# Another order of side streams and gates in a one-core layer kernel with attention, S5 and RG-LRU

## The chip, the cores and the metric

The kernel runs on one core of a Trainium2 chip. The metric is the device time of one execution in microseconds. Three runs of the kernel before gave 1795.3, 1797.18 and 1800.35 us; the median is 1797.18. Less time is better.

## The reference

One decoder layer for 2048 prompt tokens and 32 sample tokens (8 sequences of 4), all in float32, with 1024 features. One projection feeds three mixers and their gates:

```
q, k, v, g_a, u_b, g_b, x_c, g_c, g_m = split(x @ w_in)
attn = sliding-window attention(q, k, v)      # window 128, 8 query heads, 2 kv heads, sinks, bias
y_b  = S5(u_b); y_b = y_b * sigmoid(y_b @ w_glu)
y_c  = RG-LRU(causal conv4(x_c))
ya = (attn * silu(g_a)) @ w_br_a              # and yb, yc in the same way
merged = sum of sigmoid(g_m parts) * (ya, yb, yc)
y = LayerNorm(alpha * x + merged @ w_out) * ln_g + ln_b
```

The outputs are y and the new caches and states of the three mixers, for prompt and sample.

## The kernel before

**First phase.** The projection is done in 50 tiles of 128 output features: u (4), x (4), k, v, q (4), m (24, the merge gates), then the branch gates gc, gb and ga (4 each). Each tile has five units over the 2080 tokens: three of 512 columns and two of 272. A unit takes 8 slices of 128 input features, and each slice is three matmuls (mm3, lines 98 to 101), since every factor is split into a high and a low part. The result lies in a PSUM buffer mm, of which there are three. evac (line 192) empties it: for most tiles ScalarE copies it, through tanh for m, into a buffer st of the ring stage (three buffers of 128 x 512), and ScalarE's queue stores it to DRAM. For a gate tile ScalarE takes the tanh into gt, VectorE multiplies by PSUM (the first stt) and then by the mixer's output br, which gate_load (line 1371) has fetched one unit ahead, and the result in st is stored by SP's queue at the start of the next unit. gt (two buffers) and br (three) lie in a pool named gate, which attention's stream opens when it begins.

**Side streams.** The mixers are generators. tick (line 151) adds 3n/2400 to a pace after each slice of n columns; when the pace has reached the price of the last step, the next step of the first stream in the list is emitted, and the pace begins at zero. A step without a price of its own costs STEP = 4.6. All engines work in the order in which the instructions are emitted. S5 comes first; when the x tiles begin, GLU (on S5's output yD, to zD), RG-LRU (from xD, to hD) and attention (from qD, kD and vD, to aD) are appended in this order. Before gc the loop waits until attention's stream has begun, before ga until its prompt part is done, and at unit 3 of the first ga tile until all streams are done.

RG-LRU goes through four groups of 128 channels with nine steps each: five with matmuls, then Exp, Tanh, and a step with Sqrt on ScalarE and, behind it, two long multiplies and the scan on VectorE, after which SP stores hD and two states; one step is empty. GLU has eight pairs of steps, each step with 24 matmuls.

**Second phase.** The three gated branches are multiplied by their matrices (y_unit, line 1446, PSUM buffers py, four), weighted by the merge gates and summed in acc; the output projection and LayerNorm follow. BR gives the order of the branches, "cba". In the last gate branch of the first phase, seam (line 1339) fetches and splits the first branch's values (act_load, act_split) for the second phase: per unit, two raw tiles come from the pool z1 and two from stage.

**Start.** x is loaded in tiles of 128 x 512 into the ring xr (six buffers), split by ScalarE and VectorE, and kept in SBUF.

Of the kernel before, what the change touches and what calls it, by code (L numbers as in the profile page):

```python
# [9 lines left out]
FT = mybir.dt.float32  # L10
# [18 lines left out]
STEP = 4.6  # L29
# [5 lines left out]
TILES = ([("u", i) for i in range(4)] + [("x", i) for i in range(4)] + [("k", 0), ("v", 0)]  # L35
         + [("q", i) for i in range(4)]
         + [("m", i) for i in range(24)]
         + [("gc", i) for i in range(4)] + [("gb", i) for i in range(4)] + [("ga", i) for i in range(4)])
IN_NAMES = ["xT", "xr", "w_in", "w_br", "w_out", "w_glu", "lru_w", "lru_v", "lru0", "conv0",
            "s5p", "s5b", "s5c", "s5cd", "s5h", "s5hx", "s5d", "relT", "sinks", "ckT", "ck", "cv", "lnp"]  # L40
OUT_SPECS = [("y", (T, 1024)), ("kvp", (2, 128, 128)), ("ssm_p", (128, 32)), ("lru_p", (128, 4)),
# [12 lines left out]
def kernel(ctx: ExitStack, tc: tile.TileContext, I, O):  # L54
# [7 lines left out]
    def uid(p):  # L62
        cnt[0] += 1
        return f"{p}{cnt[0]}"
# [23 lines left out]
    def act(out, in_, func, scale=1.0, bias=0.0, **kw):  # L88
        return A.activation(out, in_, func, bias=bias, scale=scale, **kw)  # L89
# [24 lines left out]
    ph1 = ctx.enter_context(ExitStack())  # L114
    xlp = ph1.enter_context(tc.tile_pool(name="xl", bufs=1))
    wpool = ph1.enter_context(tc.tile_pool(name="wp", bufs=2))
    stage = ph1.enter_context(tc.tile_pool(name="stage", bufs=3))
    psum = ph1.enter_context(tc.tile_pool(name="psum", bufs=1, space=PSUM))

    def side_pool(es, name, bufs=1):  # L120
        return es.enter_context(tc.tile_pool(name=name, bufs=bufs, side="right", reuse_waits="tile"))
# [13 lines left out]

    sides, a_done, prompt_done, pace, hold = [], [False], [False], [0.0, STEP], [0]

    def side_step():  # L140
        while sides:
            try:
                r = next(sides[0])
                if r == "a":
                    a_done[0], r = True, None
                return STEP if r is None else r
            except StopIteration:
                sides.pop(0)
        return 1e9
# [42 lines left out]
    def evac(kind, i, u, ps):  # L192
        t0, n = UN[u]
        if kind == "u":
            if u == 0:
                US[i] = early.tile([128, 8, 272], FT, name=uid("us"), tag="us", bufs=2)
                G.memset(US[i][:, :, 256:272], 0.0)
            us = US[i]
            c0, nch = t0 // 8, min(n, TP - t0) // 8
            act(us[:, :, c0:c0 + nch], ps[:, :nch * 8].rearrange("p (c j) -> p j c", j=8), AF.Copy)  # L200
            if u == 4:
                smp = ps[:, 240:272].rearrange("p (b t) -> p t b", t=4)
                act(us[:, 0:4, 256:264], smp, AF.Copy)
                act(us[:, 4:8, 264:272], smp, AF.Copy)
                ST.dma_start(uD[i], us)
        elif kind == "x":
            spill(ps, n, xD[i][:, t0:t0 + n])
        elif kind in "kv":
            st = spill(ps, n, (kD if kind == "k" else vD)[:, t0:t0 + n])
            if u == 4:  # L210
                ST.dma_start(O["kvp"][0 if kind == "k" else 1], st[:, 112:240])
        elif kind == "q":
            spill(ps, n, qD[i][:, t0:t0 + n])
        elif kind == "m":
            spill(ps, n, mD[i][:, t0:t0 + n], AF.Tanh, 0.5)
        else:
            b = kind[1]
            gt = gp[0].tile([128, 512], FT, name=uid("gt"), tag="gt", bufs=2)[:, :n]
            br = gate_br.pop((b, i, u))
            act(gt, ps[:, :n], AF.Tanh, scale=0.5)  # L220
            stt(gt, gt, 1.0, ps[:, :n], OP.add, OP.mult)
            st = stage.tile([128, 512], FT, name=uid("st"), tag="st")[:, :n]
            if b == "b":
                nch = min(n, TP - t0) // 8
                V.tensor_mul(st[:, :nch * 8].rearrange("p (c j) -> p c j", j=8),
                             gt[:, :nch * 8].rearrange("p (c j) -> p c j", j=8),
                             br[:, :, 0:nch].rearrange("p j c -> p c j"))
                if u == 4:
                    V.tensor_mul(st[:, 240:272].rearrange("p (b t) -> p b t", t=4),
                                 gt[:, 240:272].rearrange("p (b t) -> p b t", t=4),  # L230
                                 br[:, 0:4, 30:38].rearrange("p t b -> p b t"))
            else:
                V.tensor_mul(st, gt, br)
            gate_st.append((actD[b][i][:, t0:t0 + n], st))
# [690 lines left out]


    def attn_stream():
        gp.append(side_pool(ges, "gate"))
        es = ExitStack()
        p = side_pool(es, "attn")  # L930
        sk = p.tile([128, 10], FT, name="sk")
# [188 lines left out]
        for n in range(34):  # L1120
            b, kv = divmod(n, 2)
# [23 lines left out]
                        load(b + 2)  # L1145
            yield ATT_SOFTMAX
        es.close()
        prompt_done[0] = True

        es = ExitStack()  # L1150
        p2 = side_pool(es, "attns")
# [74 lines left out]
        for b_ in range(8):  # L1226
            c = slice(b_ * 16, b_ * 16 + 16)
            PE.matmul(pv[:, :, b_], vc[:, b_], PT[:, :, c], start=b_ == 0, stop=False, skip_group_check=True)
        for b_ in range(8):
            c = slice(b_ * 16, b_ * 16 + 16)  # L1230
# [12 lines left out]
    early = side_pool(ees, "early")  # L1243
# [3 lines left out]
    def x_load(u):  # L1247
        t0, n = UN[u]
        for k in range(8):
            if u == 0 and k % 2 == 0:  # L1250
                kk = slice(k, k + 2)
                LD.dma_start(WR[0][:, kk], I["w_in"][0][:, kk])
            xr = early.tile([128, 512], FT, name=uid("xr"), tag="xr", bufs=6)
            LD.dma_start(xr[:, :n], I["xT"][k * 128:k * 128 + 128, t0:t0 + n])
            if u == 0 and k % 2 == 0:
                split(WS[0][0][:, kk], WS[0][1][:, kk], WR[0][:, kk])
            split(X[u][0][:, k], X[u][1][:, k], xr[:, :n])
# [1 line left out]
    x_load(0)  # L1259
    WS[1] = tuple(wpool.tile([128, 8, 128], FR, name=uid("w1"), tag=t) for t in ("wh", "wl"))  # L1260
    for kk in (slice(0, 4), slice(4, 8)):
        r = early.tile([128, 512], FT, name=uid("xr"), tag="xr", bufs=6).rearrange("p (k c) -> p k c", k=4)
        LD.dma_start(r, I["w_in"][1][:, kk])
        split(WS[1][0][:, kk], WS[1][1][:, kk], r)
    w_load(2)
# [13 lines left out]
    gp = []  # L1279
    ges = ExitStack()  # L1280


    BR = "cba"
    SCL = {"a": 0.5, "b": 0.125, "c": 0.5}
    MB = {"a": 0, "b": 8, "c": 16}
    ACT_, WB, WR2, TH, AR = {}, {}, {}, {}, {}
# [12 lines left out]
    def act_load(bi, c, k, st=False):  # L1299
        t0, n = UN[c]  # L1300
        r = raw_tile(bi == 0, st)[:, :n]
        AR[bi, c, k] = r
        LD.dma_start(r, actD[BR[bi]][k][:, t0:t0 + n])

    def act_split(bi, c, k):
# [9 lines left out]
        t = ACT_[bi, c]  # L1315
        split(t[k], t[4 + k], AR.pop((bi, c, k)), SCL[BR[bi]])

    def wb_load(j):
        if j < 24:
            bi, m = divmod(j, 8)  # L1320
            WR2[bi, m] = r = z1[0].tile([128, 4, 128], FT, name=uid("wbr"), tag="wbr", bufs=1)
            LD.dma_start(r, I["w_br"]["abc".index(BR[bi]), m])

# [8 lines left out]
    def th_load(bi, m, c, tag="br"):  # L1332
        t0, n = UN[c]
        TH[bi, m, c] = th = gp[0].tile([128, 512], FT, name=uid(tag), tag=tag, bufs=3 if tag == "br" else 2)[:, :n]
        LD.dma_start(th, mD[MB[BR[bi]] + m][:, t0:t0 + n])

# [31 lines left out]

    gate_br, gate_st = {}, []

    def gate_load(b, i, u):
        t0, n = UN[u]
        br = gp[0].tile([128, 512], FT, name=uid("br"), tag="br", bufs=3)
        if b == "b":
            c0, nch = t0 // 8, 38 if u == 4 else n // 8
            br = br[:, :8 * nch].rearrange("p (j c) -> p j c", j=8)
            LD.dma_start(br, zD[i][:, :, c0:c0 + nch])
        else:
            br = br[:, :n]
            LD.dma_start(br, (hD if b == "c" else aD)[i][:, t0:t0 + n])  # L1380
        gate_br[(b, i, u)] = br

    UORD = [3, 4, 0, 1, 2]
    for i in range(2, len(TILES)):
        kind, ti = TILES[i]
        if kind == "x" and ti == 0:
            while not a_done[0]:
                side_step()
            ees.close()
            hold[0] = 0  # L1390
            sides += [glu_stream(), lru_stream(), attn_stream()]
        if kind == "gc":
            while not gp:
                side_step()
        if kind == "ga":
            while not prompt_done[0]:
                side_step()
        if kind[0] == "g" and ti == 0:
            gate_load(kind[1], ti, 0)
        order = UORD if i == len(TILES) - 1 else list(range(5))  # L1400
        for p, u in enumerate(order):
            while gate_st:
                LD.dma_start(*gate_st.pop(0))
            if (kind, ti, p) == ("ga", 0, 3):
                while sides:
                    side_step()
            if kind[0] == "g" and (p < 4 or ti < 3):
                nxt = order[p + 1] if p < 4 else UORD[0] if i == len(TILES) - 2 else 0
                gate_load(kind[1], ti + (p == 4), nxt)
            ps = gemm(i, u)  # L1410
            if p == 0:
                w_split(i + 1)
            if p == 1:
                w_load(i + 2)
            evac(kind, ti, u, ps)
            if kind == "ga":
                seam(ti, u)
            hold[0] = int(a_done[0] and kind == "u")
            tick(UN[u][1])
# [139 lines left out]
    gb = lnp.tile([128, 2, 1024], FT, name="lngb")  # L1559
# [108 lines left out]
```

## Time and profile before

| | |
|---|---|
| median of three runs | 1797.18 us |
| the profiled execution's own time | 1798.88 us |
| its span, first to last instruction | 1797.1 us |
| mean granted TensorE clock | 0.997 |
| TensorE busy, matmuls | 1775.0 us (99%) |
| TensorE weight loads | 1549.5 us (86%) |
| VectorE busy | 1130.8 us (63%) |
| ScalarE busy | 653.8 us (36%) |
| GpSimd busy | 167.9 us (9%) |
| DMA | 220.36 MB, mean 123 GB/s |

Busy time of TensorE is the union of its matmuls' records, whose ends are modelled and overlap. Time that an engine sat idle is given before an instruction, with what released it. SP's queue issues most loads; ACTq is ScalarE's own queue of DMAs. The granted clock is 1.00 at 2.4 GHz and near 0.5 at 1.2 GHz.

### The profile page before, as it was taken

The numbers are of one execution on the slowest core, as the hardware profiler recorded it, in microseconds if no ns is written. First come the engines' busy times: TensorE is split into PE (matmuls) and PEld (weight loads), VectorE is DVE, ScalarE is ACT, GpSimd is POOL, SyncE is SP. The second block draws the span as 40 slices with busy tenths as digits, with TensorE's granted clock in tenths as the row PEclk, the third lists the DMA queues.
The fourth block names the chain that finished last, engine by engine and source line by source line (L and its number), as shares of the span: only waits on it lengthen the run. The fifth ranks groups of instructions, "written<-read, shape, count | busy, mean of one in ns | idle before, by whom it ended". The sixth has DMA issues, their size and how long they took to land. (4 is left out here: it accounts for less than half of the span.)

```text
span 1797.1 us, 26615 instructions
## 1 busy us (share of the span) xinstructions
PE 1775.0 (99%) x9788; PEld 1549.5 (86%) x9788; DVE 1130.8 (63%) x2450; ACT 653.8 (36%) x1382; POOL 167.9 (9%) x377
## 2 busy tenths in 40 slices
PE   8999999999999999999999999999999999999998
PEld 7888888888899888888988888888888888888886
DVE  5755888886334456653777899654343557666666
ACT  6312443343333287674565655311220202111110
POOL 0000000000000000000355555400000000000000
PEclk9999999999999999999999999999999999999999
DMA  7443333433333334443332334453455646542222
GB/s 235 111 135 100 111 109 112 116 108 92 120 120 114 101 93 123 104 103 95 103 104 85 119 120 134 106 165 101 143 176 155 185 137 189 186 140 94 94 94 77
DMA packets 214038, 220.36 MB, mean 123 GB/s; under 512 B 89125, under 2 KB 156709, under 8 KB 212741
## 3 DMA queue, kind: packets, MB, share of 16 engines
q1 hardware_dynamic: 182532, 169.27, 33.2%
q10 hardware_dynamic: 31376, 49.39, 7.8%
q8 instruction: 77, 1.26, 0.3%
q14 instruction: 53, 0.43, 0.1%
HBM read 136.53 MB, written 83.14 MB: 122 GB/s over the span
## 5 line engine op out<-in xcount | busy, mean ns | idle before, releaser
L99 PE MATMUL mm<-xh,wh 128*128 128x512 f32 (+1 forms) x1920 | 678.9, 354 | 0.0
L101 PE MATMUL mm<-xh,wl 128*128 128x512 f32 (+1 forms) x1920 | 673.5, 351 | 0.0
L100 PE MATMUL mm<-xl,wh 128*128 128x512 f32 (+1 forms) x1920 | 671.4, 350 | 0.0
L101 PEld LDWEIGHTS mm<-xh,wl 128*128 128x128 f32 x1920 | 361.5, 188 | 47.0 <-DVE wl L94 0.3
L99 PEld LDWEIGHTS mm<-xh,wh 128*128 128x128 f32 x1920 | 362.0, 189 | 43.4
L100 PEld LDWEIGHTS mm<-xl,wh 128*128 128x128 f32 x1920 | 362.1, 189 | 42.9
L99 PE MATMUL py<-ah,wbh 128*128 128x512 f32 (+1 forms) x480 | 168.9, 352 | 1.5 <-DVE acc L104 1.5
L101 PE MATMUL py<-ah,wbl 128*128 128x512 f32 (+1 forms) x480 | 168.9, 352 | 0.0
L100 PE MATMUL py<-ah,wbh 128*128 128x512 f32 (+1 forms) x480 | 168.8, 352 | 0.0
L89 ACT ACTIVATE st<-mm 128x512 f32<-128x512 f32 (+1 forms) x170 | 86.9, 511 | 157.2 <-PE mm L101 146.2
L99 PEld LDWEIGHTS py<-ah,wbh 128*128 128x128 f32 x480 | 90.2, 188 | 14.7 <-issue 1.9
L100 PEld LDWEIGHTS py<-ah,wbh 128*128 128x128 f32 x480 | 90.3, 188 | 12.8
L101 PEld LDWEIGHTS py<-ah,wbl 128*128 128x128 f32 x480 | 90.2, 188 | 12.5
L94 DVE TENSOR_TENSOR wl<-wr,wh 128x1024 fp32r<-128x1024 f32 x48 | 58.9, 1226 | 38.1 <-ACT wh L89 38.0
L104 DVE SCALAR_TENSOR_TENSOR gt<-gt,mm 128x512 f32<-128x512 f32 (+1 forms) x60 | 35.0, 584 | 71.1 <-ACT gt L89 70.9
L104 DVE SCALAR_TENSOR_TENSOR br<-br,py 128x512 f32<-128x512 f32 (+1 forms) x80 | 46.9, 586 | 50.9 <-PE py L101 42.5
L89 ACT ACTIVATE gt<-mm 128x512 f32<-128x512 f32 (+1 forms) x60 | 30.9, 515 | 114.4 <-PE mm L101 114.4
L89 ACT ACTIVATE wbh<-wbr 128x512 fp32r<-128x512 f32 x24 | 15.1, 629 | 147.7 <-PE py L100 125.6
L89 ACT ACTIVATE wh<-wr 128x1024 fp32r<-128x1024 f32 x48 | 50.5, 1052 | 23.8 <-DMA wr<-in_w_in_dram 14.5
L104 DVE SCALAR_TENSOR_TENSOR zy<-zs,zy 128x528 f32<-128x528 f32 x16 | 11.3, 709 | 75.4 <-ACT zs L89 75.4
L104 DVE SCALAR_TENSOR_TENSOR acc<-br,py 128x512 f32<-128x512 f32 (+1 forms) x38 | 22.1, 588 | 46.2 <-PE py L101 37.8
L1492 PE MATMUL po<-woh,mg 128*128 128x512 f32 x128 | 49.8, 389 | 0.0
(347 smaller groups left out, 2916.5 us busy)
## 6 DMA issues: line engine op xcount, KB each, us to landing
wr<-in_w_in_dram SPq DMA_DIRECT2D x48, 512.0 KB
mD<-st ACTq DMA_DIRECT2D x72, 256.0 KB
br<-mD SPq DMA_DIRECT2D x71, 256.0 KB
lx<-in_xr_dram SPq DMA_DIRECT2D x16, 512.0 KB
mD<-st ACTq DMA_DIRECT2D x48, 136.0 KB
br<-mD SPq DMA_DIRECT2D x47, 136.0 KB
xr<-in_xT_dram SPq DMA_DIRECT2D x24, 256.0 KB
wbr<-in_w_br_dram SPq DMA_DIRECT2D x24, 256.0 KB
```

What stands on the lines that cost most here:

```text
L89: return A.activation(out, in_, func, bias=bias, scale=scale, **kw)
L94: V.tensor_sub(lo, src, hi)
L99: PE.matmul(ps, wh, xh, start=start, stop=False)
L100: PE.matmul(ps, wh, xl, start=False, stop=False)
L101: PE.matmul(ps, wl, xh, start=False, stop=stop)
L104: return (eng or V).scalar_tensor_tensor(out, a, s, b, op0=op0, op1=op1)
L1492: PE.matmul(ps[c], h[:, k, :rows], wh, start=k == 0, stop=False)
```

## The change

The list of streams is now attention, RG-LRU, GLU (S5 is still ahead of them), and the gate tiles come as ga, gc, gb. BR, the order of branches in the second phase, is "acb", so that the first branch there is again that of the gates done first. Before the first ga tile at most two streams may be left, before gc one, before gb none. gb is now the branch beside which the seam runs.

The pool gate is opened only when gb begins. Until then, gate_tile takes br and gt from the ring stage, and the product is written into gt itself, in place of a tile st. stage has four buffers instead of three, and xr five instead of six.

```diff
-         + [("gc", i) for i in range(4)] + [("gb", i) for i in range(4)] + [("ga", i) for i in range(4)])
+         + [("ga", i) for i in range(4)] + [("gc", i) for i in range(4)] + [("gb", i) for i in range(4)])
...
-    stage = ph1.enter_context(tc.tile_pool(name="stage", bufs=3))
+    stage = ph1.enter_context(tc.tile_pool(name="stage", bufs=4))
...
-            gt = gp[0].tile([128, 512], FT, name=uid("gt"), tag="gt", bufs=2)[:, :n]
+            early_ = not gp
+            gt = gate_tile("gt")[:, :n]
             br = gate_br.pop((b, i, u))
             act(gt, ps[:, :n], AF.Tanh, scale=0.5)
             stt(gt, gt, 1.0, ps[:, :n], OP.add, OP.mult)
-            st = stage.tile([128, 512], FT, name=uid("st"), tag="st")[:, :n]
+            st = gt if early_ else stage.tile([128, 512], FT, name=uid("st"), tag="st")[:, :n]
...
     def attn_stream():
-        gp.append(side_pool(ges, "gate"))
...
-            xr = early.tile([128, 512], FT, name=uid("xr"), tag="xr", bufs=6)
+            xr = early.tile([128, 512], FT, name=uid("xr"), tag="xr", bufs=5)
...
-    BR = "cba"
+    BR = "acb"
...
+    def gate_tile(tag):
+
+        if not gp:
+            return stage.tile([128, 512], FT, name=uid("st"), tag="st")
+        return gp[0].tile([128, 512], FT, name=uid(tag), tag=tag, bufs=3 if tag == "br" else 2)
+
     def gate_load(b, i, u):
         t0, n = UN[u]
-        br = gp[0].tile([128, 512], FT, name=uid("br"), tag="br", bufs=3)
+        br = gate_tile("br")
...
-            sides += [glu_stream(), lru_stream(), attn_stream()]
-        if kind == "gc":
-            while not gp:
+            sides += [attn_stream(), lru_stream(), glu_stream()]
+        if kind[0] == "g" and ti == 0:
+
+            while len(sides) > {"a": 2, "c": 1, "b": 0}[kind[1]]:
                 side_step()
-        if kind == "ga":
-            while not prompt_done[0]:
-                side_step()
+            if kind == "gb":
+                gp.append(side_pool(ges, "gate"))
...
-            if (kind, ti, p) == ("ga", 0, 3):
-                while sides:
-                    side_step()
...
-            if kind == "ga":
+            if kind == "gb":
                 seam(ti, u)
```

## Rows read from the trace of the kernel before

**Rows 1.** Windows: stretch, length, busy us (instructions) per engine, clock, DMA share, GB/s.

```profile
850.00:875.00 25.00, 23.55 (x137) 20.98 (x136) 16.66 (x47) 14.20 (x43) 3.45 (x7) 0.93 0.40 126
875.00:1015.00 140.00, 139.66 (x858) 125.19 (x857) 106.98 (x235) 86.34 (x266) 76.20 (x151) 1.00 0.30 94
1015.00:1175.00 160.00, 154.33 (x906) 135.88 (x905) 133.09 (x271) 78.30 (x239) 78.51 (x154) 0.99 0.43 127
1250.00:1330.00 80.00, 80.00 (x439) 70.38 (x438) 31.20 (x55) 20.18 (x39) 0.00 (x0) 1.00 0.48 153
```

**Rows 2.** TensorE's waits, 1015 to 1175: us in total, times, longest.

```profile
PE sc L1052 <- DVE S L1012: 2.4, 4, 1.1
PE sb L1100 <- POOL ptl L1082: 1.8, 3, 1.2
PE sb L1100 <- POOL pth L1082: 0.7, 1, 0.7
PE sc L1052 <- ACT oo L89: 0.7, 1, 0.7
```

**Rows 3.** Timeline of TensorE: start, duration, instruction, idle before it; GLU and seam.

```profile
511.06 0.29 PE L99 MATMUL sa<-zh,gluh 128*128 128x264 f32 x1
...
1337.00 0.39 PE L101 MATMUL py<-ah,wbl 128*128 128x512 f32 x1
1338.88 0.47 PE L99 MATMUL py<-ah,wbh 128*128 128x512 f32 x1 [1.50 <-DVE acc L104]
```

**Rows 4.** Windows, just after the seam's wait.

```profile
1340.00:1342.00 2.00, 2.00 (x11) 1.59 (x10) 0.44 (x1) 0.00 (x0) 0.00 (x0) 1.00 0.82 208
```

**Rows 5.** Instructions on tile gt: duration ns min/median/max, first and last start, forms.

```profile
L104 DVE SCALAR_TENSOR_TENSOR gt<-gt,mm x60: 416/678/690, 1017.6 to 1336.7; 128x512 f32<-128x512 f32 x36, 128x272 f32<-128x272 f32 x24
L233 DVE TENSOR_TENSOR st<-gt,br x40: 441/691/1033, 1018.4 to 1337.4; 128x512 f32<-128x512 f32 x24, 128x272 f32<-128x272 f32 x16
L225 DVE TENSOR_TENSOR st<-gt,br x20: 591/1066/1435, 1141.2 to 1236.4; 128x512 f32<-128x512 f32 x12, 128x272 f32<-128x272 f32 x4, 128x240 f32<-128x240 f32 x4
```

**Rows 6.** Timeline of ScalarE: RG-LRU's last Sqrt, attention's first cast.

```profile
824.11 0.60 ACT L89 ACTIVATE st<-mm 128x512 f32<-128x512 f32 x1 [2.29 <-PE mm L101]
...
826.39 1.97 ACT L89 ACTIVATE R<-R 128x2104 f32<-128x2104 f32 x1
...
832.58 0.40 ACT L89 ACTIVATE st<-mm 128x272 f32<-128x272 f32 x1 [2.31 <-PE mm L101]
...
835.60 0.40 ACT L89 ACTIVATE st<-mm 128x272 f32<-128x272 f32 x1 [2.63 <-PE mm L101]
...
851.07 0.63 ACT L89 ACTIVATE q<-qr 64x512 fp32r<-64x512 f32 x1 [9.42 <-DMA qr<-qD]
```

**Rows 7.** Timeline of VectorE: GLU, RG-LRU's last scan, the seam.

```profile
509.59 1.26 DVE L96 SCALAR_TENSOR_TENSOR zl<-zy,zh 128x1056 fp32r<-128x1056 f32 x1 [1.15 <-ACT zh L89]
...
828.39 2.35 DVE L104 SCALAR_TENSOR_TENSOR R<-a,R 128x2104 f32<-128x2104 f32 x1 [10.01 <-ACT R L89]
...
833.37 4.54 DVE L914 TENSOR_TENSOR_SCAN R<-a,xf 128x2104 f32<-128x2104 f32 x1
...
1325.39 0.69 DVE L233 TENSOR_TENSOR st<-gt,br 128x512 f32<-128x512 f32 x1 [5.16 <-DMA actDa<-st]
```

**Rows 8.** Timeline of SP's queue: start, duration of the issue, DMA.

```profile
456.25 0.92 SPq L724 DMA_DIRECT2D zy<-in_w_glu_dram  x2
...
843.03 0.60 SPq L951 DMA_DIRECT2D qr<-qD  x1
...
1320.40 0.42 SPq L1403 DMA_DIRECT2D actDa<-st  x1
```

**Rows 9.** What SP's queue waited for, 465 to 615: us in total, times, longest.

```profile
SPq L688 <- DMA zD<-zy: 15.6, 6, 2.6
```

**Rows 10.** DMA beside the gb tiles, 1135 to 1240.

```profile
DMA packets 27474, 14.11 MB, mean 134 GB/s; under 512 B 21453, under 2 KB 25005, under 8 KB 27453
```

**Rows 11.** What SP's queue waited for at the start, 0 to 60.

```profile
SPq L1254 <- DVE xl L94: 15.9, 22, 3.8
```

More of the change, by code (lines that the diff above doesn't have):

```diff
@@ L134 @@
         X[u] = (xhp.tile([128, 8, n], FR, name=f"xh{u}", tag=f"xh{u}"), xlp.tile([128, 8, n], FR, name=f"xl{u}"))
-    sides, a_done, prompt_done, pace, hold = [], [False], [False], [0.0, STEP], [0]
+    sides, a_done, pace, hold = [], [False], [0.0, STEP], [0]
     def side_step():
@@ L1147, in attn_stream @@
         es.close()
-        prompt_done[0] = True
         es = ExitStack()
@@ L1261 @@
     for kk in (slice(0, 4), slice(4, 8)):
-        r = early.tile([128, 512], FT, name=uid("xr"), tag="xr", bufs=6).rearrange("p (k c) -> p k c", k=4)
+        r = early.tile([128, 512], FT, name=uid("xr"), tag="xr", bufs=5).rearrange("p (k c) -> p k c", k=4)
         LD.dma_start(r, I["w_in"][1][:, kk])
```

## The prediction

> **What bounds the kernel now.** I read the page first: TensorE is busy 99% of the span, so only the places where TensorE waits, or runs at its lower clock, can be won or lost. The windows by stage come next [rows 1]: the reader is to compare TensorE's busy time with the length of each stretch. Attention beside the merge tiles (875 to 1015) loses 0.34 us in 140. Attention beside the gates (1015 to 1175) loses 5.67 us in 160, with VectorE at 133 of 160. Attention's first steps (850 to 875) lose 1.45 us, and the granted clock is 0.93 there. The view of waits names who is late in the gate stretch [rows 2]: nine waits, all in attention's own matmuls, on VectorE (S), on GpSimd, which follows VectorE, and on ScalarE. The last loss before the second phase is one wait of 1.50 us in the seam [rows 3]. What is not a wait of TensorE is hidden.
>
> An idle time in the trace is shorter than the delay. Two matmuls that stand 1.88 us apart show 1.50 us idle [rows 3]; the pace is 0.227 us (a unit of 512 columns is 24 matmuls in 5.45 us, one of 272 takes 3.02 us [rows 6]), so the delay is 1.65 us. I add 0.15 us per wait.
>
> **Where the streams lie.** Each k-slice of a projection unit adds 3n/2400 us to the pace; a step comes when its price is reached, and the overshoot is lost, so a step of 4.6 takes 5.0 on average. I counted yields with these rules; a tile is 20.8 pace-us. S5 ends at 363.8 in either order (m tile 3). Before: GLU to 472, RG-LRU to 660, attention to 965; the gates begin at 790.4, so gc and gb ran beside attention, and ga beside nearly nothing. After: attention 364 to 664, wholly beside m tiles; RG-LRU 664 to 852.5, so that its last 12 of 38 steps lie beside ga; GLU 852.5 to 956.5, beside ga's last tile and gc; gb, from 956.8, is alone. None of the new drains forces a step. For the count speaks that it puts RG-LRU's last scan of before into the unit of 512 columns ahead of two of 272, where ScalarE's rows show it [rows 6].
>
> **Attention off the gates.** In the gate stretch: 5.67 us idle, 9 waits by 0.15 (1.4), clock 0.99 over 160 us (1.6) [rows 1, 2], together 8.7. Beside m tiles, by the 0.34 us per 140, the same work costs 0.4. Gain 8.3, between 5 (GpSimd's own chain stays) and 8.7. What is late next there is nothing that the m stretch shows. The first steps: attention's qr load was issued at 843.03 because SP was held by the RG-LRU outputs behind the scan that ended at 837.9, and ScalarE waited for it until 851.07 [rows 6 to 8]. After S5, SP issues the next stream's loads at 456.25, some 3.5 us after the step [rows 8]; attention's first cast comes three steps (some 16 us) after its loads, and 8 us for the landing, as at 843, then fits. So 1.45 us idle, 0.3 for two waits and 25 x 0.07 = 1.75 of clock go: 3.5; nothing of it if the load is late again. Sum: -11.8 (-5 to -12.2).
>
> **RG-LRU beside ga.** An m tile gives its PSUM buffer back when ScalarE has read it; a gate tile only when VectorE's multiply has, and VectorE works in order. RG-LRU's step after the Sqrt holds VectorE without a break: two operations of 2.35 us, the scan of 4.54 us, small ones between. In the trace this runs from 828.39 to 837.9, and the unit ahead ended at 824.1 [rows 6, 7]. So VectorE is free 13.8 us after that unit's end; without the store issue that ScalarE has there, some 13.4. By the count two such steps lie beside ga: in tile 0 at unit 2 and in tile 2 at unit 3. At the first the blocked unit has 512 columns and two of 272 follow: TensorE fills the three buffers in 5.45 + 3.02 + 3.02 = 11.5 us and then needs the first one, which comes at 13.4 + 0.68 [rows 5] = 14.1: 2.6 us. At the second (272, 272, 512) the same 11.5 against 13.9: 2.4. With 0.1 us for each release: 5.2. Queued behind on VectorE are the three gates' multiplies and RG-LRU's next split; on SP, behind the 1 MB store of hD, the gate loads, and these have three units of slack. A wait of 1.65 us left the clock at 1.00 [rows 3, 4]; waits of 1.45 us with little work between them, at 850, cost 1.75 us of clock [rows 1]. The two new ones are longer than either: I take the 1.75 for both. Sum +8.7; bounds 0 (a release I overlook) and 8.7 plus 2 x 4 (a gate load late behind hD).
>
> **GLU beside ga's end and gc.** GLU's chain is thin already: zl ends at 510.85 and TensorE reads it from 511.06 [rows 3, 7]. A gate puts 0.68 + 0.69 us on VectorE per unit [rows 5], but these stand in order ahead of the step, done 2 us into a unit, while the step's matmuls end after 3.6 or later. SP is held some 2.6 us per pair by GLU's own load behind its store [rows 9]; gate stores, gate loads and weight loads queue behind it, with a unit to spare. I take +1.0, for the start (w_glu behind hD), with 0 and 8.8 as ends.
>
> **The seam.** Now gb lies at it. Its multiply takes 1.07 instead of 0.69 us [rows 5], with 0.21 more once per tile, and its loads are strided. On the other hand stage has 4 buffers. In the last tile each unit draws three (gate, two raw tiles), so with 3 the gate's result falls on the buffer whose store SP has just issued: store 1320.40, multiply 1325.39 [rows 7, 8]. With 4 it falls on a raw tile that is split already. I followed the last five units: gate multiplies no longer wait, the splits and next loads come some 4 us sooner by the third unit, and the first py buffer is freed near 1333, where 1337.2 would do. Even with 5 x 0.4 us of slower multiplies the 1.65 us go: -1.65 (-1.65 to +5).
>
> **The rest.** xr with 5 buffers: SP waited 15.9 us for xr's splits with 6 [rows 11]; one buffer less moves each later load by one split (0.67 us); the second unit has hardly a spare one: +0.5 (0 to 1.5). Gates beside streams draw br and gt from stage: two per unit, so a load waits for the multiply of two units before, ahead of which SP already waited to store its result: 0 (0 to 1). gb's first load waits for zD's last store, some 3 us [rows 9]; covered by its first unit. gt as its own output, the order of branches in the second phase: the same instructions, 0.
>
> **Sum.** -11.8 + 8.7 + 1.0 - 1.65 + 0.5 = -3.3 us. Against the profiled execution (span 1797.1, its time 1798.88, which is 1.7 above the median): 1795.6; against the median 1797.18: 1793.9, so 1794.
>
> **A rule that speaks against it.** The loads of gb lie in pieces below 512 bytes, 21453 of 27474 packets in its stretch, and 134 GB/s were moved there, against 153 beside the aD loads [rows 1, 10]: 12% less. The Trainium skill (DMA: Bandwidth & Descriptors, Specifications) wants at least 512 B for line rate, since smaller transfers are read, modified and written; the rows agree in direction. By that rule the seam would grow, which is the third rival.
>
> **Rivals.**
> 1. The scan bursts cost nothing or little: the clock stays up (1.75 x 2 less) or the release comes sooner. For it: a 1.65 us wait left the clock alone [rows 4]. Against: the order on VectorE. -3.3 - 3.5 to -3.3 - 8.7, so 1790 to 1785; 0.28.
> 2. GLU's thin chain breaks: a late gate load holds VectorE, and each of the 8 pairs starts late by a gate's 1.37 us less the 0.2 spare. It decides once a gate's pair stands between zs and zl. 8 x 1.1 = 8.8 instead of 1.0: +4.5, and a loss of clock with some of them, 1802 to 1806; 0.12.
> 3. The seam is held by z loads: if each of the last four gate multiplies comes 1.4 us later (0.4 its own, 1.0 of load), the 1.65 stay and 5.5 come: -3.3 + 1.65 + 5.5 = +3.9, 1801; 0.10.
> 4. Attention's waits are its own and follow it: its gain is 3.5 in place of 11.8. Against it stands the 875 to 1015 row. +5.0, 1802; 0.06.
> The forecast has the remaining 0.44, with its own range 1790 to 1798.
>
> **Chances.** A measurement here tells 0.3%, 5.4 us, from no change. Faster by more: most of rival 1 and a little of the forecast, 0.32. Slower by more: most of rival 2, a part of 3 and 4, and the open ends of SP's queue, 0.17. Same 0.51. The range 1784 to 1804 takes in rival 1 whole, 3, 4 and half of 2.
>
> **What would show it.** Right: no waits on S, ptl or pth in the view of waits but in the first half; two waits of mm's first matmul on VectorE's gt in ga, each 2 to 3 us, behind a scan, followed by a granted clock near 0.55; no wait of py on acc. Wrong: waits of sa or sb in gc (rival 2), py waiting on acc for several us (3), waits on S or ptl beside m tiles (4), or no wait in ga at all (1).

## The result, and the profile after

The median after is 1809.24 us of 6 runs (1807.01 to 1812.74), against 1797.24 us of 6 runs before: a ratio (of the means) of 1.0064, 95% interval 1.0051 to 1.0076. The change makes the kernel slower by 12.0 us; 1794 was predicted, with 1804 as the upper end. The profiled execution after has a span of 1808.3 us, 11.2 more than before.

First the windows of the kernel after, with the columns of [rows 1]; the first seven cut the program by stage, the last three look closer.

```profile
450.00:825.00 375.00, 374.64 (x2232) 332.28 (x2231) 238.34 (x527) 187.54 (x564) 152.78 (x312) 1.00 0.31 97
825.00:850.00 25.00, 25.00 (x126) 22.06 (x125) 8.45 (x47) 4.27 (x10) 0.00 (x0) 0.86 0.31 91
850.00:1015.00 165.00, 164.60 (x872) 142.49 (x871) 94.21 (x129) 115.73 (x169) 0.30 (x3) 1.00 0.41 108
1015.00:1060.00 45.00, 37.24 (x192) 32.06 (x191) 30.91 (x43) 21.82 (x36) 0.00 (x0) 0.89 0.47 101
1085.00:1130.00 45.00, 38.32 (x192) 32.00 (x191) 25.20 (x34) 12.17 (x18) 0.00 (x0) 0.96 0.56 165
1130.00:1250.00 120.00, 120.00 (x775) 110.30 (x774) 63.71 (x80) 40.69 (x55) 0.00 (x0) 1.00 0.42 136
1250.00:1345.00 95.00, 95.00 (x516) 83.20 (x516) 47.76 (x73) 25.98 (x48) 0.00 (x0) 1.00 0.60 163
...
842.00:846.00 4.00, 4.00 (x19) 3.65 (x19) 0.00 (x0) 1.14 (x3) 0.00 (x0) 0.56 0.11 16
...
1028.00:1036.00 8.00, 6.97 (x26) 5.26 (x25) 0.08 (x1) 0.51 (x2) 0.00 (x0) 0.86 0.72 104
1036.00:1044.00 8.00, 4.10 (x10) 3.24 (x11) 6.04 (x10) 6.82 (x11) 0.00 (x0) 0.57 0.17 50
```

Attention now lies beside the merge tiles (450 to 843) and leaves TensorE 0.36 us idle in 375, where beside the gates it left 5.67 in 160 [rows 1]. gc beside GLU from 1130, and gb alone from 1250 to 1345, leave nothing idle; the seam's 1.50 us [rows 3] are gone. The time is in two stretches, 1015 to 1060 and 1085 to 1130: 7.76 and 6.68 us idle, at clocks of 0.89 and 0.96. TensorE's timeline names who was late there (idle before the instruction, and its releaser, stand in brackets). In it mm is the projection's PSUM buffer and sa that of RG-LRU's and GLU's own matmuls; f, zh and zl are their split inputs, R and ig what ScalarE takes out of RG-LRU's sa, gluh a split part of w_glu, and st a tile of the ring, be it a gate's br, gt or result:

```profile
1025.35 0.50 PE L99 MATMUL mm<-xh,wh 128*128 128x512 f32 x1 [2.83 <-DVE st L104]
1039.90 1.22 PE L888 MATMUL sa<-f,lwh 128*128 128x512 f32 x2 [4.92 <-ACT ig L89]
...
1091.00 0.50 PE L99 MATMUL mm<-xh,wh 128*128 128x512 f32 x1 [2.58 <-DVE st L104]
1106.70 0.39 PE L99 MATMUL mm<-xh,wh 128*128 128x272 f32 x1 [2.93 <-DVE st L104]
...
1124.11 0.39 PE L100 MATMUL sa<-zl,gluh 128*128 128x264 f32 x1 [0.91 <-DVE zl L96]
```

The first and third are the two waits behind RG-LRU's scans. The second, the longest, and the fourth, at GLU's start, were not forecast at that size.

To add up such places I took, for each matmul, the time until the next one starts, less the median of its shape and program line, and summed it by stretch. A wait and a lowered clock both count in it, and so does the scatter of attention's small matmuls: of the 4.3 us from 450 to 825 after, one wait is 0.5 and no other delay is above 0.2. The last three columns are experiments 2, 7 and the first of 8 of the next section.

| stretch, us | before | after | scan split | states packed | split and packed |
|---|---|---|---|---|---|
| 0 to 450 | 6.1 | 6.4 | 7.0 | 7.4 | 7.3 |
| 450 to 825 | 1.4 | 4.3 | 4.3 | 4.3 | 4.3 |
| 825 to 850 | 0.0 | 3.4 | 3.2 | 1.9 | 3.1 |
| 850 to 1015 | 5.3 | 1.2 | 1.0 | 0.6 | 0.9 |
| 1015 to 1085 | 4.6 | 11.8 | 5.4 | 9.8 | 2.6 |
| 1085 to 1130 | 1.6 | 9.4 | 4.9 | 3.7 | 3.2 |
| 1130 to 1250 | 5.8 | 0.8 | 0.6 | 0.7 | 0.5 |
| 1250 to 1345 | 1.9 | 0.0 | 0.2 | 0.2 | 0.3 |
| 1345 to the end | 3.9 | 5.2 | 4.6 | 4.7 | 3.7 |
| sum | 30.6 | 42.4 | 31.1 | 33.2 | 26.0 |

The sums differ by 11.8 between before and after, the spans by 11.2. Each column is one execution, and the clock is not the same in each: from 1130 to 1250 before loses 5.8 at a clock of 0.99, and experiment 9's kernel, with the same waits there, 3.8 at 1.00.

Why RG-LRU's matmul that was due at 1034.6 found nothing to read is a chain over three engines. VectorE after:

```profile
1014.97 2.35 DVE L104 SCALAR_TENSOR_TENSOR R<-a,R 128x2104 f32<-128x2104 f32 x1 [1.86 <-ACT R L89]
1017.35 2.35 DVE L104 SCALAR_TENSOR_TENSOR xf<-xf,R 128x2104 f32<-128x2104 f32 x1
...
1019.95 4.54 DVE L915 TENSOR_TENSOR_SCAN R<-a,xf 128x2104 f32<-128x2104 f32 x1
...
1024.62 0.68 DVE L104 SCALAR_TENSOR_TENSOR st<-st,mm 128x512 f32<-128x512 f32 x1
1025.33 0.69 DVE L234 TENSOR_TENSOR st<-st,st 128x512 f32<-128x512 f32 x1
...
1035.92 0.44 DVE L104 SCALAR_TENSOR_TENSOR st<-st,mm 128x272 f32<-128x272 f32 x1 [8.48 <-ACT st L89]
```

From 1014.97 to 1024.52 VectorE works off the multiplies and the scan, as in [rows 7] but now with a gate's two operations behind them; its result is there at 1026.02. SP's queue after:

```profile
1024.52 0.32 SPq L918 DMA_DIRECT2D hD<-R  x1
...
1026.32 1.18 SPq L921 DMA_DIRECT2D out_lru_s_dram<-hs  x1
1027.60 0.86 SPq L1408 DMA_DIRECT2D actDa<-st  x1
1028.55 1.53 SPq L1385 DMA_DIRECT2D st<-aD  x1
1030.14 0.42 SPq L1408 DMA_DIRECT2D actDa<-st  x1
...
1097.54 0.81 SPq L725 DMA_DIRECT2D zy<-in_w_glu_dram  x2
```

The gate's store goes out at 1027.60, behind hD's 1 MB and the state stores. ScalarE after:

```profile
1035.49 0.40 ACT L89 ACTIVATE st<-mm 128x272 f32<-128x272 f32 x1 [8.99 <-DMA actDa<-st]
1035.79 1.27 ACT L89 ACTIVATE f<-xf 64x512 fp32r<-64x512 f32 x2
...
1103.22 0.63 ACT L89 ACTIVATE gluh<-zy 128x512 fp32r<-128x512 f32 x1 [11.32 <-DMA zy<-in_w_glu_dram]
```

The tanh at 1035.49 writes the ring slot that a stored tile must leave, that of two units before, and waits for the store of 1027.60 to land, some 7.9 us after its issue. Behind it in ScalarE's order stand RG-LRU's casts f and its R and ig, so TensorE's sa waits, and VectorE, which had stood 8.48 us idle, too. At GLU's start the head of ScalarE's queue is gluh, which waits for the w_glu load until 1103.22, with a gate's tanh behind it. That load is issued late because SP waits for the smallest of RG-LRU's stores, 0.5 KB of the prompt's state issued at 1091.26, to land (SP's waits, 1085 to 1100: us in total, times, longest):

```profile
SPq L725 <- DMA out_lru_p_dram<-R: 2.9, 1, 2.9
```

### The profile page after: what moved, and what is told of

The parts are those of the page before. It is cut to its first block, busy times and chain, and to the rows that moved or that the text cites. A ratio compares the mean times of both kernels' runs of the same rounds, so it can differ in the third digit from the quotient of the medians.

```text
span 1808.3 us, 26674 instructions
## 1 busy us (share of the span) xinstructions
PE 1779.4 (98%) x9788; PEld 1552.9 (86%) x9788; DVE 1131.5 (63%) x2450; ACT 654.7 (36%) x1382; POOL 162.4 (9%) x377
## 4 chain that ended last, share of the span: by engine, by line
PE 87%; DMA 4%; DVE 4%; ACT 2%; issue 1%; SPq 0%; ACTq 0%; DVEq 0%
PE mm L99 18%; PE mm L101 18%; PE mm L100 18%; PE py L99 5%; PE py L101 5%; PE py L100 5%; PE po L1496 3%; PE po L1495 3%; PE po L1494 3%; PE sb L1100 1%; DVE R L915 1%; DMA lx<-xD 1%; DMA xr<-in_xT_dram 1%; ACT R L89 1%; PE sa L1026 1%
## 5 line engine op out<-in xcount | busy, mean ns | idle before, releaser
L89 ACT ACTIVATE st<-mm 128x512 f32<-128x512 f32 (+1 forms) x210 | 107.5, 512 | 251.9 <-PE mm L101 204.6
L1494 PE MATMUL po<-woh,mo 128*128 128x512 f32 x128 | 49.8, 389 | 0.0
L1495 PE MATMUL po<-wol,mo 128*128 128x512 f32 x128 | 49.8, 389 | 0.0
L1495 PE MATMUL po<-wol,mg 128*128 128x512 f32 x128 | 49.8, 389 | 0.0
```

The costliest lines, as they stand in the source:

```text
L1494: PE.matmul(ps[c], h[:, k, :rows], wh, start=k == 0, stop=False)
L1495: PE.matmul(ps[c], h[:, k, :rows], wl, start=False, stop=False)
```

## Experiments

All on the kernel after unless said otherwise. Theories: **A**, SP's queue is held by RG-LRU's stores; **B**, VectorE's burst (multiplies and scan in one step) by itself; **C**, hD's 1 MB fills the DMA engines; **D**, ScalarE's Sqrt and table loads; **E**, which came after the first four runs, the sample states' store, which reads single elements of 4 bytes. All ratios are to the kernel before, with the 95% interval.

**1. RG-LRU's stores on GpSimd's queue.**
```diff
-            SD.dma_start(hD[i][:, :TP], R[:, :TP])
+            G.dma_start(hD[i][:, :TP], R[:, :TP])
```
(the other three stores likewise)

> Changed kernel (1809.2 us) with RG-LRU's four stores per channel group (hD twice, the two states) issued by GpSimd's queue instead of SP's. Theory A (SP's queue is held behind the scan by these stores, so gate stores, gate loads and w_glu come late, the ring stage is not freed, and ScalarE and then TensorE stand): the wait of RG-LRU's first matmuls (5.1 us at 1034.6, with the clock loss around it some 8) and the wait at GLU's start (3.1 us at 1103.4) go or shrink below 1 us each; the two waits behind the scans (3.0 and 2.7 us) stay; 1797 to 1801 us. Rival B (VectorE's burst alone is the cause, everything after it only trails behind): all four waits stay, 1807 to 1811. Rival C (the 1 MB store fills the DMA queues, whoever issues it): the 5.1 us shrink to 2 to 4, GLU's start stays, 1804 to 1808.

1813.55 us, 1.0087 (1.0064 to 1.0110): 4.3 us slower than after. The sa delay is 5.63 instead of 5.09 us, the one at GLU's start 7.31 instead of 3.09. Theory A as it was put falls, and no expectation had a slower kernel. The DMA view of this run, 1084 to 1106 us (issue, count, size, median us from issue to landing), shows something else:

```profile
hD<-R POOLq DMA_DIRECT2D x1, 1024.0 KB, 4.9
...
out_lru_s_dram<-hs POOLq DMA_DIRECT2D x1, 4.0 KB, 9.5
```

The 1 MB lands after 4.9 us, the 4 KB of states after 9.5. In the group whose stores stand ahead of the sa delay (1020 to 1034) they take 7.8 and 9.8, so this view alone does not tell the 1 MB from the pieces. The Trainium skill (DMA: Bandwidth & Descriptors, Issuing engines are not separate DMA queues) says that transfers of all issuing engines run on the same 16 DMA engines; this run agrees in that another queue did not take the load off.

**2. The scan one step behind the multiplies.** The empty step that stood behind a group is used for it.
```diff
+            yield
             V.tensor_tensor_scan(R, aa, b_, 0.0, op0=OP.mult, op1=OP.add)
...
-            if i + 1 < 4:
-                yield
```


> Changed kernel with one more yield in RG-LRU's long step, between the two multiplies and the scan (the empty step behind it is dropped, so the number of steps grows by one in all). VectorE's burst of 9.6 us becomes one of 4.7 and one of 4.8, with a gate's work between. Prediction's step on the bursts: the two waits of the projection's first matmul on VectorE (3.0 and 2.7 us) go, with a part of the clock loss behind them. Theory A adds that SP is still held until the scan, now one step later, so the wait of RG-LRU's matmuls and GLU's start stay in part: 1798 to 1804. Rival B: everything goes, 1789 to 1795. Rival D (ScalarE's Sqrt with its two table loads sets the wait, not VectorE's order): no change, 1807 to 1811.

1796.48 us, 0.9996 (0.9985 to 1.0008): 12.76 us under after, level with before. Both waits behind scans are gone, and RG-LRU's and GLU's waits remain in part:

```profile
PE sa L888 <- ACT ig L89: 3.4, 3, 2.2
PE mm L99 <- DVE st L104: 3.2, 1, 3.2
```

(In these rows: who waited for whom, us in total, times, longest.) So the burst is the root of most of the loss, also of part of the ring's. That part goes by way of SP: with the scan a step later, the gate's product of 512 columns gets between the multiplies and the scan, and its store goes out ahead of hD's instead of behind it:

```profile
1021.84 0.32 SPq L1407 DMA_DIRECT2D actDa<-st  x1
...
1026.51 0.32 SPq L919 DMA_DIRECT2D hD<-R  x1
```

What the order of these stores is worth without the split, experiment 6 shows; the 12.76 us hold both. ScalarE's Sqrt and table loads are all still there: D falls.

**3. Experiments 1 and 2 together.** 

> Both edits: the scan in a step of its own and RG-LRU's stores on GpSimd's queue. Theory A: neither wait behind the scans nor the two waits behind SP's queue is left, the attention's gain (13 us of waits and clock less than before) stands: 1788 to 1793, faster than the kernel before (1797.2). Rival B: as the split alone. Rival C: 1793 to 1798.

1797.66 us, 1.0005 (0.9993 to 1.0017), nothing beyond the split alone: the sa delays shrink (1.09, 0.91 and 0.5 us), GLU's start grows to 6.72.

**4. Gate stores on GpSimd's queue** (ga's and gc's), so that they pass hD's issue.
```diff
-                LD.dma_start(*gate_st.pop(0))
+                (LD if gp else G).dma_start(*gate_st.pop(0))
```


> Changed kernel with only the gate results' stores of ga and gc on GpSimd's queue; RG-LRU's stores, the gate loads and w_glu stay on SP's. Theory A1 (what stands is ScalarE, because the buffer of the gate two units before waits for its store behind hD): the 5.1 us wait shrinks to below 2 us, GLU's start stays: 1801 to 1805. Theory A2 (what is late is the gate load behind hD, and VectorE waits for it): the 5.1 us stay within 1 us, 1807 to 1811.

1805.70 us, 1.0046 (1.0033 to 1.0059): 3.5 us under after. The sa delay falls from 5.09 to 3.39 only; now it waits for VectorE's f, which stands behind a gate's product whose load, issued at 1028.06, came 7.7 us later:

```profile
1035.79 0.44 DVE L234 TENSOR_TENSOR st<-st,st 128x272 f32<-128x272 f32 x1 [6.93 <-DMA st<-aD]
```

GLU's start grows from 3.09 to 4.15. Neither expectation came in full: it is not the order of the issues on SP alone, the gate's load (7.7 us) is as late as its store (7.9 after).

**5. GLU's empty step ahead of the weight splits,** alone and on the split scan.
```diff
             SD.dma_start(gr[i], I["w_glu"][:, 2 * i:2 * i + 2])
         yield
+        yield
...
             yield GLU_WEIGHTS
-        yield
         gelu_a(0)
```


> The kernel after with only the GLU's empty step moved to right behind the w_glu loads; RG-LRU as in after. Theory A (order of steps at GLU's start is its own term of about 4.7 us, beside the scan's terms): the mm wait of 3.09 us at 1103 goes, the waits behind the scans (3.0 and 2.74 us) and the sa wait (5.09 us) stay, time 1805 (1804 to 1806.5). Rival (the scan of group 3 delays everything by that much anyway and the wait is handed on to the first GLU pair): the time stays at 1808 to 1810.

> The kernel after, with the scan one step behind the multiplies ahead of it (as in the experiment on the split scan) and, in the GLU stream, its empty step moved from behind the four weight splits to right behind the two w_glu loads. What is left beside gates in the split-scan run is mainly the GLU's start: TensorE's mm waits 3.37 us because ScalarE's gluh split sits at the head of its queue until the w_glu load lands, with a gate's tanh behind it. Theory A (the order of the steps: the split is queued one step too early): the wait at GLU's start falls from 3.37 to 0.7 us or less, and the time to 1793 (1791 to 1795), 3 to 4 us under the split-scan version's 1796.5. Rival (the load's lateness is handed on: gelu_a(0) is then queued before zy of group 0 has landed, or the first GLU pair waits on DVE zl instead): the wait reappears at the first GLU matmul, 2 us or more, and the time stays at 1796 to 1797.

Alone 1808.17 us, 1.0069 (1.0055 to 1.0083), and with the split 1797.68, 1.0006 (0.9995 to 1.0017): no gain, the rival was right in both. The delay at the start goes and the first GLU pair takes it over, in the run with the split:

```profile
1115.03 0.59 PE L99 MATMUL sa<-zh,gluh 128*128 128x264 f32 x1 [3.75 <-ACT zh L89]
1116.32 0.59 PE L100 MATMUL sa<-zl,gluh 128*128 128x264 f32 x1 [0.70 <-DVE zl L96]
```

The lateness is that of w_glu's landing, not of a step's place.

**6. hD's and the states' stores one step later** (groups 0 to 2).
```diff
+            if i + 1 < 4:
+                yield
             SD.dma_start(hD[i][:, :TP], R[:, :TP])
...
             yield
-            if i + 1 < 4:
-                yield
```


> The kernel after with hD's stores and the two state stores of groups 0 to 2 one step later than the scan (the empty step that stood behind them stands ahead of them); group 3 as in after. So the gate's store of the unit that the scan held goes out ahead of the 1 MB of hD and of the state store's small pieces, not behind them. Theory C (the transfers that RG-LRU's stores put ahead of the gate's store and load on the DMA engines make the sa wait): the wait of 5.09 us at 1034 falls under 1.5 us, and the time to 1804 (1802 to 1806). Rival B (VectorE's burst alone has eaten the slack, and the gate's load would be late whatever is ahead of it): the wait stays at 4 us or more, the time at 1808 to 1810. In both the waits behind the two scans (3.0 and 2.74 us) and the GLU's start stay.

1802.89 us, 1.0037 (1.0025 to 1.0049): 6.4 us under after. The sa delay is gone; the waits behind the scans (3.02 and 2.74) and GLU's start (2.62) stay. ScalarE of this run at the place of the 8.99 us:

```profile
1027.64 0.40 ACT L89 ACTIVATE st<-mm 128x272 f32<-128x272 f32 x1 [2.42 <-DMA actDa<-st]
```

So it is the transfers that RG-LRU puts ahead of the gate's store and load; B alone does not explain the wait. Whether the 1 MB or the small pieces, this run leaves open.

**7. The sample states packed before their store.**
```diff
-            SD.dma_start(O["lru_s"][:, i], hs[:, :, 3])
+            hc = p.tile([128, 8], FT, name=uid("hc"), tag="hc")
+            V.tensor_copy(hc, hs[:, :, 3])
+            SD.dma_start(O["lru_s"][:, i], hc)
```


> The kernel after with the sample states hs[:, :, 3] copied on VectorE into a tile of 8 columns before their 4 KB store, which reads 8 single elements (4 bytes each, 32 bytes apart) from each of the 128 partitions in after. In after's trace the stretch 1028 to 1036 us holds 1,346 packets under 512 bytes and 0.83 MB with the DMA engines busy 71% of it, at 104 GB/s, and 1091 to 1098 us 1,360 such packets at 183 GB/s, against 264 GB/s in the 4 us of the 1 MB store before. Theory E (these small pieces, not hD's 1 MB, make the transfers beside them late): packets under 512 bytes fall by about 900 in each stretch, the sa wait of 5.09 us falls to 1 to 3 us, w_glu lands 1 to 3 us earlier, and the time is 1804 (1802 to 1806.5). Rival C (the 1 MB of hD): waits and time as in after, 1808 to 1810. Rival B (VectorE's burst alone): as in after too.

1801.59 us, 1.0030 (1.0019 to 1.0041): one copy of 128x8 and one DMA of the same 4 KB in another form take 7.65 us off. From 1025 to 1036 us the DMA engines had, after:

```profile
DMA packets 2049, 1.89 MB, mean 172 GB/s; under 512 B 1408, under 2 KB 1664, under 8 KB 1920
```

and with the states packed:

```profile
DMA packets 1409, 2.03 MB, mean 184 GB/s; under 512 B 544, under 2 KB 928, under 8 KB 1312
```

That is 864 packets under 512 B less (1,024 single elements, which lie 16 bytes apart in hs and not 32, become 128 rows, 896 less). The Trainium skill (DMA: Bandwidth & Descriptors, Rules for kernel authors) says that a strided last dimension becomes one descriptor per element and should be made contiguous; the packet counts agree (1408 to 544 under 512 B). The gate's store is there when the tanh starts, 3.8 us after its issue instead of 7.9, and the tanh comes 5.1 us earlier (hD's store is 0.9 of that earlier):

```profile
1026.64 0.40 SPq L1410 DMA_DIRECT2D actDa<-st  x1
...
1030.43 0.40 ACT L89 ACTIVATE st<-mm 128x272 f32<-128x272 f32 x1 [4.60 <-DMA actDa<-st]
```

hD's 1 MB is unchanged, so C falls as the main cause, and E stands; what the 1 MB has in the 2.32 us that are left of the 5.09 of sa, no run separates. w_glu is issued 4.3 us behind hD's store instead of 7.1 and lands sooner. Not all of the gain is waits: from 1015 to 1130 the table loses 7.7 us less, of which the single delays are 3.3. The rest is clock, granted at 1.00 in both stretches of this profile, although the waits behind the scans are as long as after's (3.20 and 2.94 us of delay); why it did not fall here is not shown.

**8. Split and packing together, and two variants.** In the second variant ga's and gc's stores go through GpSimd as in experiment 4; in the first the conv states' store is packed like the sample states:
```diff
-                SD.dma_start(O["conv_s"][:, i], smp[:, :, 4:7])
+                cc = p.tile([128, 8, 3], FT, name=uid("cc"), tag="cc")
+                V.tensor_copy(cc, smp[:, :, 4:7])
+                SD.dma_start(O["conv_s"][:, i], cc)
...
-            hs = p.tile([128, 8, 4], FT, name=uid("hs"), tag="hs", bufs=2)
+            hs = p.tile([128, 8, 4], FT, name=uid("hs"), tag="hs")
```
(hs, which holds the sample's results, gives up one of its two buffers to make room)

> The kernel after with both: the scan one step behind its multiplies, and the sample states packed into 8 adjacent columns before their store. The packing alone took 7.6 us from after (1809.2 to 1801.6), the split alone 12.7 (to 1796.5). Theory E (what the split leaves, sa waits of 1.09 and 2.41 us and the GLU's start of 3.37 us, hangs on the small pieces ahead of the gates' stores and of w_glu): these fall by 3 to 5 us together, the time to 1792 (1790 to 1794). Rival (both mends free the same slack, and what the split leaves is the 1 MB of hD and the ring): 1795.5 to 1797.

> The split and the packed sample states, and the conv states' store (3 elements of 4 bytes out of every 7, 1,024 pieces of 12 bytes a group) packed the same way; hs has one buffer in place of two to make room. Theory E (small pieces next to gates cost): 0.5 to 2 us under the version with the sample states alone. Rival (the conv store is issued where no gate's store or load is late): equal to it within 1 us.

> The split and the packed sample states, with ga's and gc's gate stores on GpSimd's queue in place of SP's. If what is left of the waits beside RG-LRU and at the GLU's start is the gate's store queued behind other SP work, 1 to 2 us under the version without it; if it is the gate's load or the DMA engines themselves, within 1 us of it or up to 2 us slower (hD's stores on that queue made the GLU's start later, 7.3 us against 3.1).

Together: 1793.23 us of 11 runs, 0.9979 (0.9970 to 0.9988), 16.0 us under after and faster than before. TensorE's waits of that run:

```profile
PE sa L888 <- ACT ig L89: 2.2, 3, 1.2
PE mm L99 <- DVE st L104: 1.2, 1, 1.2
PE sa L100 <- DVE zl L96: 0.9, 1, 0.9
```

With the gate stores on GpSimd: 1792.07 us of 8 runs, 0.9972 (0.9961 to 0.9982); the 1.2 us between the two are within what the intervals leave open. It has the lowest median of all versions.

With the conv states packed too: 1807.46 us, 1.0061 (1.0049 to 1.0074), 14 us worse, which neither expectation had. The copy stands on VectorE at the place where only SP had waited for the load:

```profile
878.05 0.18 DVE L834 COPY cc<-lx 128x24 f32<-128x24 f32 x1 [4.78 <-DMA lx<-xD]
878.26 1.40 DVE L867 TENSOR_TENSOR f<-xf,f 64x512 fp32r<-64x512 f32 x2
```

RG-LRU's next f is behind it in VectorE's order, and TensorE's sa waits for that f (7.5 us in five waits, and 2.6 in two more behind ScalarE; how the rest of the 14 us divides is not shown). The single buffer of hs was not tried alone, but no engine waits on hs in RG-LRU of this trace.

**9. The packing alone on the kernel before.** 

> The kernel before, its order of streams untouched, with only the packing of the sample states. Theory E' (the pieces hurt only where gates draw their tiles from the ring and from SP's loads while RG-LRU runs, which is so in after and not in before): 1796 to 1798, no change. Rival (they cost before as well, at the first attention step at 852 us, which stands behind the last RG-LRU group's stores): the waits of 1.24 and 0.54 us there go and the time falls to 1793 to 1795.

1797.66 us, 1.0003 (0.9994 to 1.0011): no change. In its profiled execution (1794.39 us) the wait at attention's first step is gone, the stretch 850 to 1015 loses 2.2 us in place of 5.3; but its 11 runs reach from 1794.35 to 1799.58, as before's do (1794.37 to 1800.76), and the median does not show it. Attention's first q is cast 5.2 us after its load's issue (843.21 to 848.45), where before it was 8.0 (843.03 to 851.07 [rows 6, 8]): the pieces held up a load there, too. By the medians the pieces cost only where a gate's tiles depend on stores landing while RG-LRU runs: in the new order.

## Why the prediction was wrong

- **Attention off the gates, -11.8: the mechanism right, the size in part luck.** In the table before loses 17.3 us from 850 to 1250 (5.3 + 4.6 + 1.6 + 5.8, with attention [rows 1, 2]), and after 4.3 from 450 to 825: -13.0. In experiment 9's profile, with attention's first wait gone and the clock at 1.00, the same stretches lose 12.6, which would make it -8.3. The 8 us that the term took for a load to land were 5.2 without the states' pieces (experiment 9). No wait on ptl or pth is left, and one on S of 0.4 us. What I had not seen is the 3.4 us of lowered clock behind attention's end (825 to 850).
- **RG-LRU's scans beside ga, +8.7: the waits right, the rest short.** 2.6 and 2.4 us were predicted, 3.00 and 2.74 came, in the units named, and the split took them away. Clock: 1.75 us for each were put in, 3.5 together. From 1015 to 1130 the table has 21.2 us, of which the seven single delays named here are 15.9; some 5.3 are left for the clock, behind more waits than these two.
- **"Gates beside streams draw br and gt from stage: ... 0 (0 to 1)": the step that failed.** I followed the load, which waits for a multiply. But gt takes its tile from the ring too and is itself the tile that is stored; so ScalarE's tanh waits until a store of two units before has landed, with RG-LRU's casts queued behind it. In the term on the scans the gate loads' "three units of slack" was taken as safe cover, although the scan takes it (experiment 4). Measured: 5.09 + 0.36 us of delay, and clock. That the store is there only 7.9 us after its issue is owed mostly to 4 KB of states in 1,024 pieces (packed, it is 3.8), which the sum did not hold at all.
- **GLU's start, +1.0 (ends 0 and 8.8): mis-sized.** The place was right, w_glu behind RG-LRU's stores, but SP waits there not for hD but for 0.5 KB among the pieces to land, and the delays are 3.09 at the start and 0.43 + 1.17 in the first pair: 4.7 us, and clock. The chain of GLU's later pairs held, as forecast; rival 2 did not come.
- **The seam, -1.65: right** (1.9 lost before from 1250 to 1345, 0.0 after). **xr, +0.5:** 0.3 in the table, and 0.9 to 1.3 in its last three columns, whose kernels start alike: within its range.
- **The sum.** RG-LRU and GLU were to cost 9.7 and cost 21.8 (1.2 + 11.8 + 9.4 + 0.8 in after, less 1.4 in before). With -13.0, -1.9, +3.4 at 825 and +1.6 at both ends that makes 11.9, the 11.8 of the table but for rounding. None of the rivals was this one; the nearest was the upper bound of the scan term, "a gate load late behind hD", to which I gave too little weight.

That one term is not independent of the next is seen in the returns: the split gives 12.76 us back, the packing 7.65, both 16.01, not 20.41. Not tried is the ring itself: gates with tiles of their own beside RG-LRU and GLU. So its share in the loss is read from the traces and from what shortens the store, not from a run that takes the wait away.

## What to carry to other kernels

When evacuations draw from a ring whose tiles are also stored, count the slot's life until its store has landed, and name what stands behind the instruction that takes it; slack that covers one late step is spent when a long operation and a slow transfer fall into the same units. Look at each small store beside a tight ring for single elements: here 4 KB took longer to land than 1 MB (9.5 against 4.9 us in experiment 1), and what was issued behind them was late with them. And before a copy is put on an in-order engine, ask what the copy waits for.

## What the runs showed that was not expected

Behind attention's 32 small matmuls at 839.3 to 843.4 (128x32 and 4x32, no idle time in TensorE) the granted clock stood at 0.56 from 842 to 846, which is the lower level, 1.2 GHz, for most of it. In the run of experiment 3 the same instructions left it at 1.00:

```profile
842.00:846.00 4.00, 4.00 (x32) 3.83 (x32) 0.00 (x0) 1.14 (x3) 0.00 (x0) 1.00 0.11 16
```

The loss at 825 to 850 was 0.4, 1.9 or 3.1 to 3.4 us in twelve of the profiled executions; no run here shows what decides between them.
